# A hybrid decoder layer on one core: buffers and banks laid out anew across three stages, and the first of seven products in three float32r parts

## The chip, the cores and the metric

The kernel runs on one core of a Trainium2 chip. The metric is the device time of one execution in microseconds. Three runs of the kernel before took 2590.86, 2594.02 and 2598.33 us; the median is 2594.02 us.

## The reference

One decoder layer is computed for a prompt of 512 tokens and for 8 samples of 4 tokens, 544 columns in all (NT). The parts that matter here are the dense products:

```
h    = rmsnorm(x) @ w_in           # 2048 -> 6160, split into the heads
y    = concat(o_a, o_b) @ w_out    # gated linear attention | dilated attention
x    = x + y
up   = rmsnorm(x) @ w_ffn_up       # 2048 -> 2 * 5504
conv = causal depthwise conv of width 3 over up; u, g = its two halves
x    = x + (silu(g) * u) @ w_ffn_down
out  = rmsnorm(x)
```

Everything is float32, with states, caches and the last rows of `up` as further outputs.

## The kernel before, in words

**Layout and split products.** Activations lie transposed: 128 features in the partitions, 544 tokens along the row; HT = 272 is half of that. A float32 product is made of float32r matmuls: each operand is split into a high part (ScalarE copies to float32r, L190) and a low part (VectorE subtracts, L191), and three products are added in PSUM: high by high, high by low, low by high (`gemm`, L219 to L226). A weight unit is 8 tiles of 128 x 128 (512 KB): the SP queue loads it into `raw`, `split` makes `whi` and `wlo` from it. A plain product over 16 k has two units and, for two halves of columns, 96 matmuls.

**Who sets the order.** The program is written in Python and a planner orders each engine's instructions by priority and by the times it expects; each engine then runs its list in order. Weight loads and splits stand in `tc.high_priority` (offset PO = 4000), so they are issued ahead of the products that use them, as far as buffers allow. Memory is handed out from two stacks of pools (left and right); a pool opened where another lay waits for the work of the old one.

**The stages.** The in-projection with both attentions fills the time up to about 886 us; its weights go through the pool `wts` (three `raw`, three `whi`, three `wlo`; `wunit`, L196 to L217), its products through the PSUM pool `psg` (two buffers `g` of two banks each), and small products through `pss`. After the last gates (L802 to L805) the attention outputs `o[k]` are split into `og[k]` (L847 to L849, in the order 10 to 15, then 0 to 9). At L810 `wts` is closed and `wu` is opened in its place, with three `raw` and four `whi` and `wlo`.

*Output projection* (L891 to L910): 16 output tiles of 96 matmuls, each added to x (L899), written to `hscr`, squared for the norm, scaled by the norm's weights (L908). For the next stage `factors` (L872 to L888) forms from each pair of tiles (a row pair i, eight in all) seven right-hand blocks: B11, B21, B22 and the sums T1 to T4, each with a high part `vh` and a low part `vl`; four row pairs during the stage, four after it (in `VB`, where the activations lay). B11 is kept as a plain float32 block `v11`.

*Up-projection* (L954 to L1089): 43 pairs f, a tile of the u half and one of the g half. A pair is a 2 x 2 block product done with seven products instead of eight (Strassen's scheme, in Winograd's form) over 8 row pairs, 272 columns each. `p1` is A11 x B11 as 8 full float32 matmuls (`product1`, L941); the other six, `p5`, `p6`, `p2`, `p7`, `p3`, `p4`, are 24 float32r matmuls each (`product`, L934) with a weight split each. The left operands are sums: s = A21 + A22 by a second, adding DMA of the POOL queue (L968); s += A11 on VectorE for p6 (L988); s += A12 for p3 (L998). PSUM holds `b0` (p1, p6, p7, p4 in turn), `z` (p5, p3) and `y` (p2), two buffers each, in `psu`. `p1` of pair f + 1 stands between `p7` and `p3` of pair f; p1 of pair 0 stands in the loop, after the norm's statistics (`rms_stat`, L915) and after `rstdF` and `vcv`. A pair ends with the convolution (L1032 to L1046) and the gated product, which goes to the DRAM scratch `adr`, or stays in SBUF as a kept tile for three pairs.

*Down-projection* (L1093 to L1222): PSUM is opened anew with three buffers `g` and two `v`. First 16 short products of the three kept tiles (18 matmuls), evacuated by ScalarE (L1129), while `fetch` (L1111) brings the other tiles back; then groups of 16, 16 and 8 tiles, the final norm and the output.

Of the kernel before, what the change touches and what calls it, by code (L numbers as in the profile page):

```python
# [9 lines left out]
F32 = mybir.dt.float32  # L10
F32R = mybir.dt.float32r
# [6 lines left out]
P = 128  # L18
# [4 lines left out]
TS = 4  # L23
# [100 lines left out]
def _build(tc, nc, es, xT, st_gla, ck, cv, conv_in, vecs, w_in, w_gu, w_out, w_up, w_dn,  # L124
# [36 lines left out]
    eps = cons.tile([P, 1], F32, name="eps")  # L161
    zs = cons.tile([2 * RANK, NT], F32, name="zs")
    rstd = cons.tile([P, NT], F32, name="rstd")
# [645 lines left out]

    closed(wts_p)  # L810
    wu_p, wu = opened(name="wu", bufs=1, side="right")


    def wsplit(raw, n=8):

        hi = wu.tile([P, 8, P], F32R, tag="whi", name="whi", bufs=4)
        lo = wu.tile([P, 8, P], F32R, tag="wlo", name="wlo", bufs=4)
        split(hi[:, :n], lo[:, :n], raw[:, :n])
        return hi, lo
# [22 lines left out]
    def wraw():  # L842
        return wu.tile([P, 8, P], F32, tag="raw", name="raw", bufs=3)

# [6 lines left out]

    va_p, VA = opened(name="va", bufs=1, side="right")
    hx_p, HX = opened(name="hx", bufs=1, side="right")
    hscr = [dram.tile([P, NT], F32, name=f"hscr{k}") for k in range(KD)]
# [3 lines left out]

    B21, B22, T1, T2, T3, T4 = range(6)
    NV = 6  # L860
    vh, vl, v11 = [None] * (KD // 2), [None] * (KD // 2), [None] * (KD // 2)

# [9 lines left out]
    def factors(some, X, pool):  # L872
        for i in some:
            vh[i] = pool.tile([P, NV, HT], F32R, name=f"vh{i}")
            vl[i] = pool.tile([P, NV, HT], F32R, name=f"vl{i}")
            v11[i] = pool.tile([P, HT], F32, name=f"v{i}")
            nc.scalar.activation(v11[i], X[i][:, 0, :HT], AF.Copy)
        for i in some:
            b11, b12, b21, b22 = X[i][:, 0, :HT], X[i][:, 0, HT:], X[i][:, 1, :HT], X[i][:, 1, HT:]
            t = HX.tile([P, 2, HT], F32, tag="ts", name="ts", bufs=1)  # L880
            u = HX.tile([P, 2, HT], F32, tag="tu", name="tu", bufs=1)
            nc.vector.tensor_sub(t[:, 0], b11, b12)
            nc.vector.scalar_tensor_tensor(t[:, 1], t[:, 0], -1.0, b22, op0=OP.mult, op1=OP.subtract)
            parts(i, T1, 2, t)
            nc.vector.tensor_sub(u[:, 0], b22, b12)
            nc.vector.scalar_tensor_tensor(u[:, 1], t[:, 1], -1.0, b21, op0=OP.mult, op1=OP.subtract)
            parts(i, T3, 2, u)
            parts(i, B21, 2, X[i][:, 1].rearrange("p (a c) -> p a c", a=2))  # L888

    X = {}  # L890
    for ot in range(KD):  # L891
# [17 lines left out]
        if j == 1 and i < AHEAD:  # L909
            factors([i], X, VA)  # L910
    closed(acts_p)
    ra_p, RA = opened(name="ra", bufs=2)
    vb_p, VB = opened(name="vb", bufs=1)
    factors(list(range(AHEAD, KD // 2)), X, VB)
    rms_stat(acc2, rstd, htmp)  # L915
    closed(hx_p, pss, psg)

    g0_p, G0 = opened(name="g0", bufs=NKEPT, side="right")
    fp_p, FP = opened(name="ffn", bufs=1, side="right")
    psu_p, pu = opened(name="psu", bufs=1, space=PSUM)  # L920
    rstdF = FP.tile([P, FW], F32, name="rstdF")
    nc.vector.memset(rstdF, 1.0)
    nc.scalar.activation(rstdF[:, 2:2 + TP], rstd[:, :TP], AF.Copy)
    nc.scalar.activation(rstdF[:, 2 + TP:].rearrange("p (b s) -> p b s", s=2 + TS)[:, :, 2:],
                         rstd[:, TP:].rearrange("p (b t) -> p b t", t=TS), AF.Copy)
    vcv = FP.tile([P, NVEC - V_CW], F32, name="vcv")
    nc.gpsimd.dma_start(vcv, vecs[:, V_CW:])
    wv = w_up.rearrange("(k t p) c -> t p k c", t=2, p=P)
# [11 lines left out]

    def product1(b, a):  # L941
        for i in range(8):
            nc.tensor.matmul(b[:, :HT], a[:, i, :], v11[i], start=(i == 0), stop=(i == 7), skip_group_check=True)  # L943

    def tmp(name):
        return FP.tile([P, HT], F32, tag=name, name=name, bufs=1)

# [6 lines left out]
    class Pair:  # L954
# [5 lines left out]
        def load(self, *parts, tag=None):  # L960

            x = RA.tile([P, 8, P], F32, tag=tag, name=tag) if tag else wraw()
            for n, (side, t) in enumerate(parts):
                c0 = side * FF + self.f * P
                if n == 0:
                    nc.sync.dma_start(x, wv[t][:, :, c0:c0 + P])
                else:
                    nc.gpsimd.dma_start(x, wv[t][:, :, c0:c0 + P], accum_op=OP.add)  # L968
            return x

        def p1(self):
            with ahead():
                self.a11 = self.load((0, 0), tag="ra")
            self.b0 = pu.tile([P, 512], F32, tag="b0", name="b0", bufs=2)
            product1(self.b0, self.a11)
            self.V = tmp("V")
            nc.scalar.activation(self.V, self.b0[:, :HT], AF.Copy)

        def p5(self):
            with ahead():  # L980
                self.s = self.load((1, 0), (1, 1), tag="rs")
                A = wsplit(self.s)
            self.z = pu.tile([P, 512], F32, tag="z", name="z", bufs=2)
            product(self.z, A, T1)
# [9 lines left out]
        def p2(self):  # L994
            with ahead():
                self.a12 = self.load((0, 1))
                A = wsplit(self.a12)
                nc.vector.tensor_add(self.s, self.s, self.a12)  # L998
            y = pu.tile([P, 512], F32, tag="y", name="y", bufs=2)
            product(y, A, B21)  # L1000
# [31 lines left out]
        def conv(self):  # L1032
# [13 lines left out]
            return out  # L1046

    ci_v = conv_in.rearrange("p (s f) r -> p s f r", s=2)
    co_v = conv_out.rearrange("p (s f) r -> p s f r", s=2)
# [5 lines left out]
    ci = co = None  # L1055
    pairs = [Pair(f) for f in range(KF)]
    for f, pr in enumerate(pairs):
# [5 lines left out]
        pr.ci, pr.co = ci[:, :, f % 4, :], co[:, :, f % 4, :]  # L1063
        if f == 0:
            pr.p1()
        pr.p5()
# [20 lines left out]
        if f % 4 == 3 or f == KF - 1:  # L1087
            f4 = f - f % 4
            nc.gpsimd.dma_start(co_v[:, :, f4:f + 1, :], co[:, :, :f + 1 - f4, :])  # L1089
    closed(fp_p, vb_p, ra_p, psu_p)  # L1090


    rows_p, rows = opened(name="rows", bufs=KD)  # L1093
    ds_p, DS = opened(name="ds", bufs=NSLOT)
    psd_p, pg = opened(name="psd", bufs=3, space=PSUM)
    psv_p, pS = opened(name="psv", bufs=2, space=PSUM)

    def vps():
        return pS.tile([P, 512], F32, tag="v", name="v")

    def gps():
        return pg.tile([P, 2, 512], F32, tag="g", name="g")

# [21 lines left out]
    for ot in range(KD):  # L1125
# [3 lines left out]
        nc.scalar.activation(hv(h[ot]), ps[:, :, :HT], AF.Copy)  # L1129
    closed(g0_p, va_p)  # L1130
    ds2_p, DS2 = opened(name="ds2", bufs=24 - NSLOT, side="right")
# [3 lines left out]
    def wraw():  # L1135
        even[0] ^= 1
        if even[0]:
            return wu.tile([P, 8, P], F32, tag="raw", name="raw", bufs=3)
        return W3.tile([P, 8, P], F32, tag="raw3", name="raw3", bufs=2)
# [73 lines left out]
    for s in range(2):  # L1213
# [5 lines left out]
        for ot in range(KD):  # L1219
            eng = nc.gpsimd if ot % 3 == 2 else nc.vector  # L1220
            eng.tensor_mul(h[ot][:, c], h[ot][:, c], rstd[:, c])
            (nc.sync if ot % 2 else nc.scalar).dma_start(yT[ot * P:(ot + 1) * P, c], h[ot][:, c])  # L1222
    closed(w3_p, ds2_p, ds_p, rows_p, wu_p, psv_p, psd_p)

# [65 lines left out]
```

## Time and profile before

| | |
|---|---|
| median of three runs | 2594.02 us |
| the profiled execution | 2600.62 us, span of the profile 2598.8 us |
| mean granted TensorE clock | 0.985 |
| TensorE, VectorE, ScalarE, GpSimd busy | 97%, 60%, 40%, 17% of the span |
| bytes moved by DMA | 427.67 MB, mean 165 GB/s |

PE is TensorE, PEld its weight loads, DVE VectorE, ACT ScalarE, POOL GpSimd, SP the engine that issues most loads; a name with a q (SPq) is an engine's queue of issues. L with a number is a line of the kernel before. The granted clock is a share of 2.4 GHz; 0.50 is the level of 1.2 GHz. A full float32 matmul stands as two records in the trace, a float32r one as one. In rows of the form "out<-in" buffer numbers are left out, so `g` is any of the PSUM buffers of that name.

### The profile page before, as it was taken

The numbers are of one execution on the slowest core, as the hardware profiler recorded it, in microseconds if no ns is written. First come the engines' busy times: TensorE is split into PE (matmuls) and PEld (weight loads), VectorE is DVE, ScalarE is ACT, GpSimd is POOL, SyncE is SP. The second block draws the span as 40 slices with busy tenths as digits, with TensorE's granted clock in tenths as the row PEclk, the third lists the DMA queues.
The fourth block names the chain that finished last, engine by engine and source line by source line (L and its number), as shares of the span: only waits on it lengthen the run. The fifth ranks groups of instructions, "written<-read, shape, count | busy, mean of one in ns | idle before, by whom it ended". The sixth has DMA issues, their size and how long they took to land.

```text
span 2598.8 us, 46302 instructions
## 1 busy us (share of the span) xinstructions
PE 2515.1 (97%) x19135; PEld 2390.4 (92%) x19135; DVE 1570.1 (60%) x2381; ACT 1030.5 (40%) x1777; POOL 452.3 (17%) x592
## 2 busy tenths in 40 slices
PE   7999999999999699979999999999999999999997
PEld 7988877899998599979999999999999999999997
DVE  7877753267767644277777777777777653342244
ACT  5344454133334433244444444444444441131142
POOL 4433333300002300012122212121211000000001
PEclk9999999999999899989999999999999999999999
DMA  7777634622222253379999999999988384353332
GB/s 206 203 204 202 184 108 116 167 75 80 60 77 63 81 148 114 99 164 238 269 242 271 244 268 244 272 243 271 243 185 183 93 242 116 110 157 90 90 90 70
DMA packets 581588, 427.67 MB, mean 165 GB/s; under 512 B 18976, under 2 KB 553728, under 8 KB 580608
## 3 DMA queue, kind: packets, MB, share of 16 engines
q1 hardware_dynamic: 462144, 248.31, 34.7%
q0 software_dynamic: 115200, 171.02, 28.8%
q10 hardware_dynamic: 4032, 5.38, 0.6%
q8 instruction: 150, 2.46, 0.4%
q14 instruction: 62, 0.51, 0.1%
HBM read 397.40 MB, written 77.37 MB: 183 GB/s over the span
## 4 chain that ended last, share of the span: by engine, by line
PE 86%; DMA 6%; DVE 4%; issue 1%; ACT 1%; POOL 0%; SPq 0%; DVEq 0%; POOLq 0%; ACTq 0%
PE g L225 42%; PE b L938 15%; PE z L938 10%; PE b L943 6%; PE y L938 5%; DMA q<-qscr 4%; PE s L660 1%; PE v L507 1%; DMA ar<-adr 1%; PE s L555 1%; PE s L542 1%; DVE pr L411 1%; PE s L778 0%; PE s L781 0%; DMA rs<-in_w_up_dram 0%
## 5 line engine op out<-in xcount | busy, mean ns | idle before, releaser
L190 ACT ACTIVATE whi<-raw 128x1024 fp32r<-128x1024 f32 (+1 forms) x345 | 356.0, 1033 | 702.0 <-PE g L225 470.4
L191 DVE TENSOR_TENSOR wlo<-raw,whi 128x1024 fp32r<-128x1024 f32 (+1 forms) x341 | 408.2, 1198 | 216.7 <-ACT whi L190 208.4
L225 PE MATMUL g<-ah,whi 128*128 128x272 f32 x2048 | 442.4, 295 | 22.2 <-DMA raw<-in_w_out_dram 19.5
L225 PE MATMUL g<-ah,wlo 128*128 128x272 f32 x2048 | 442.9, 294 | 0.3 <-DVE wlo L191 0.3
L225 PE MATMUL g<-al,whi 128*128 128x272 f32 x2048 | 442.9, 295 | 0.0
L225 PEld LDWEIGHTS g<-ah,whi 128*128 128x128 f32 x2048 | 326.6, 190 | 36.9 <-ACT whi L190 22.0
L225 PEld LDWEIGHTS g<-ah,wlo 128*128 128x128 f32 x2048 | 328.1, 191 | 12.2 <-issue 10.1
L225 PEld LDWEIGHTS g<-al,whi 128*128 128x128 f32 x2048 | 327.8, 191 | 12.1 <-issue 10.4
L938 PE MATMUL b<-vh,whi 128*128 128x272 f32 x1032 | 306.3, 297 | 1.3 <-ACT V L1013 1.3
L938 PE MATMUL b<-vh,wlo 128*128 128x272 f32 x1032 | 296.9, 288 | 0.0
L938 PE MATMUL b<-vl,whi 128*128 128x272 f32 x1032 | 296.6, 287 | 0.0
L225 PE MATMUL g<-dh,whi 128*128 128x272 f32 x1248 | 258.5, 289 | 3.3 <-ACT whi L190 2.1
L225 PE MATMUL g<-dl,whi 128*128 128x272 f32 x1248 | 257.9, 288 | 0.0
L225 PE MATMUL g<-dh,wlo 128*128 128x272 f32 x1248 | 257.8, 288 | 0.0
L190 ACT ACTIVATE whi<-rs 128x1024 fp32r<-128x1024 f32 x129 | 135.9, 1054 | 193.8 <-PE b L938 123.6
L191 DVE TENSOR_TENSOR wlo<-rs,whi 128x1024 fp32r<-128x1024 f32 x129 | 157.7, 1222 | 84.5 <-ACT whi L190 84.5
L938 PE MATMUL z<-vh,whi 128*128 128x272 f32 x688 | 207.0, 301 | 0.0
L225 PEld LDWEIGHTS g<-dh,whi 128*128 128x128 f32 x1248 | 195.3, 188 | 4.2 <-ACT whi L190 2.5
L938 PE MATMUL z<-vh,wlo 128*128 128x272 f32 x688 | 198.5, 289 | 0.0
L938 PE MATMUL z<-vl,whi 128*128 128x272 f32 x688 | 198.1, 288 | 0.0
L938 PEld LDWEIGHTS b<-vh,whi 128*128 128x128 f32 x1032 | 194.9, 189 | 3.2 <-ACT V L1013 1.5
L938 PEld LDWEIGHTS b<-vl,whi 128*128 128x128 f32 x1032 | 194.4, 188 | 1.6
(347 smaller groups left out, 4699.0 us busy)
## 6 DMA issues: line engine op xcount, KB each, us to landing
raw<-in_w_up_dram SPq DMA_DIRECT2D x129, 512.0 KB, 5.4
raw<-in_w_in_dram SPq DMA_DIRECT2D x96, 512.0 KB, 4.3
raw<-in_w_dn_dram SPq DMA_DIRECT2D x64, 512.0 KB, 4.2
out_k_s_dram<-in_ck_dram POOLq DMA_DIRECT2D x8, 3060.0 KB, 17.0
out_v_s_dram<-in_cv_dram POOLq DMA_DIRECT2D x8, 3060.0 KB, 17.5
raw<-in_w_up_dram POOLq DMA_DIRECT2D x43, 512.0 KB, 7.7
ra<-in_w_up_dram SPq DMA_DIRECT2D x43, 512.0 KB, 7.6
rs<-in_w_up_dram SPq DMA_DIRECT2D x43, 512.0 KB, 6.4
```

The costliest lines, as they stand in the source:

```text
L190: nc.scalar.activation(hi, src, AF.Copy)
L191: eng.tensor_sub(lo, src, hi.bitcast(F32))
L225: nc.tensor.matmul(ps[:, s, :HT], a, b[:, s * HT:(s + 1) * HT], start=(i == 0 and n == 0), stop=(i == len(todo) - 1 and n == 2))
L411: nc.vector.tensor_mul(pr, kt[:, 4:5, :].broadcast_to([P, TS, QC]), q5[:, 1:5, :])
L507: nc.tensor.matmul(psv[32 * m:32 * m + 32, :QC], lhs, rhs, start=(kt == 0), stop=(kt == 5), tile_position=(0, 32 * m))
L542: nc.tensor.matmul(psc[:, :n], q[r, qi * P:(qi + 1) * P], k[r, :n], start=True, stop=True)
L555: nc.tensor.matmul(psc[r, :P], vt[:, j * P + 64 * e:j * P + 64 * e + 64], t[:, j * P:(j + 1) * P], start=(j == 0), stop=(j == qi))
L660: nc.tensor.matmul(ps[:, c * P:(c + 1) * P], KS[:, c * P:(c + 1) * P], Q[:, :, c * 64:(c + 1) * 64], start=True, stop=True)
L938: nc.tensor.matmul(b[:, :HT], a_[:, i, :], x_[i][:, v, :], start=(first and i == 0 and n == 0), stop=(i == 7 and n == 2), skip_group_check ...
L943: nc.tensor.matmul(b[:, :HT], a[:, i, :], v11[i], start=(i == 0), stop=(i == 7), skip_group_check=True)
```

## The change

1. Weight tiles stay in one pool: `wts` is not closed at L810, and out-, up- and down-projection take `raw`, `whi` and `wlo` from it. The ring of `whi` and `wlo` is three deep there, where `wu` had four. `wu` keeps only p1's and the other products' temporaries `V` and `U`.
2. PSUM: `psg` with its two buffers `g` stays open to the end. `pss` is closed before the output projection and `psu` opened there, with one `v` and two `b0`. In the up-projection z and y are the two halves of one `g`. The down-projection has two `g` where it had three, and one `v` where it had two.
3. B11 is split like the other blocks (seven blocks in `vh` and `vl`), and `p1` becomes a `product` of 24 float32r matmuls with a weight split of A11. `product1` and `v11` go.
4. The tiles `ra` and `rs` of a pair come from `RE` (even pairs) or `RA` (odd pairs), one buffer each, where `RA` had two of each. `RE` is opened on the right before the output projection.
5. `p1` of pair 0 moves ahead of `rms_stat`, and with it ahead of `rstdF` and the load of `vcv`; these now stand after the class `Pair`.
6. `zs` moves from `cons` to `rowsB`.

```diff
-    zs = cons.tile([2 * RANK, NT], F32, name="zs")
+    zs = rowsB.tile([2 * RANK, NT], F32, name="zs", bufs=1)
...
-    closed(wts_p)
     wu_p, wu = opened(name="wu", bufs=1, side="right")
...
-        hi = wu.tile([P, 8, P], F32R, tag="whi", name="whi", bufs=4)
-        lo = wu.tile([P, 8, P], F32R, tag="wlo", name="wlo", bufs=4)
+        hi = wts.tile([P, 8, P], F32R, tag="whi", name="whi")
+        lo = wts.tile([P, 8, P], F32R, tag="wlo", name="wlo")
...
     def wraw():
-        return wu.tile([P, 8, P], F32, tag="raw", name="raw", bufs=3)
+        return wts.tile([P, 8, P], F32, tag="raw", name="raw", bufs=3)
+
+    closed(pss)
+    psu_p, pu = opened(name="psu", bufs=1, space=PSUM)
+
+    def vps():
+        return pu.tile([P, 512], F32, tag="v", name="v")
...
     va_p, VA = opened(name="va", bufs=1, side="right")
+    re_p, RE = opened(name="re", bufs=1, side="right")
     hx_p, HX = opened(name="hx", bufs=1, side="right")
...
-    B21, B22, T1, T2, T3, T4 = range(6)
-    NV = 6
+    B11, B21, B22, T1, T2, T3, T4 = range(7)
+    NV = 7
...
-            v11[i] = pool.tile([P, HT], F32, name=f"v{i}")
-            nc.scalar.activation(v11[i], X[i][:, 0, :HT], AF.Copy)
+            parts(i, B11, 1, X[i][:, 0, :HT].unsqueeze(1))
...
-    ra_p, RA = opened(name="ra", bufs=2)
+    ra_p, RA = opened(name="ra", bufs=1)
     vb_p, VB = opened(name="vb", bufs=1)
     factors(list(range(AHEAD, KD // 2)), X, VB)
-    rms_stat(acc2, rstd, htmp)
-    closed(hx_p, pss, psg)
...
     def tmp(name):
-        return FP.tile([P, HT], F32, tag=name, name=name, bufs=1)
+        return wu.tile([P, HT], F32, tag=name, name=name, bufs=1)
...
-            x = RA.tile([P, 8, P], F32, tag=tag, name=tag) if tag else wraw()
+            x = (RA if self.f % 2 else RE).tile([P, 8, P], F32, tag=tag, name=tag) if tag else wraw()
...
                 self.a11 = self.load((0, 0), tag="ra")
+                A = wsplit(self.a11)
             self.b0 = pu.tile([P, 512], F32, tag="b0", name="b0", bufs=2)
-            product1(self.b0, self.a11)
+            product(self.b0, A, B11)
...
-            self.z = pu.tile([P, 512], F32, tag="z", name="z", bufs=2)
+            self.g = gps()
+            self.z = self.g[:, 0]
             product(self.z, A, T1)
...
-            y = pu.tile([P, 512], F32, tag="y", name="y", bufs=2)
+            y = self.g[:, 1]
             product(y, A, B21)
...
+    pairs = [Pair(f) for f in range(KF)]
+    pairs[0].p1()
+    rms_stat(acc2, rstd, htmp)
+    closed(hx_p)
...
-        if f == 0:
-            pr.p1()
         pr.p5()
...
-    psd_p, pg = opened(name="psd", bufs=3, space=PSUM)
-    psv_p, pS = opened(name="psv", bufs=2, space=PSUM)
```

## Rows read from the trace of the kernel before

**Rows 1.** The page, part 1: busy time of each engine.

```profile
PE 2515.1 (97%) x19135; PEld 2390.4 (92%) x19135; DVE 1570.1 (60%) x2381; ACT 1030.5 (40%) x1777; POOL 452.3 (17%) x592
```

**Rows 2.** Waits of PE: who waited for whom, us in total, times, longest.

```profile
PE g L225 <- DMA raw<-in_w_out_dram: 19.5, 1, 19.5
PE b L943 <- DVE rs L169: 7.7, 1, 7.7
PE v L325 <- DVE acc L906: 7.0, 1, 7.0
```

**Rows 3.** The chain that ended last, both seams: start us, us, what.

```profile
906.03 195.99 PE g L225 x1536
1102.45 5.46 DMA rs<-in_w_up_dram
1109.03 6.44 DMA rs<-in_w_up_dram
1121.67 6.57 PE b L943 x16
1128.24 3.02 PE z L938 x24
```

**Rows 4.** Windows: both holes, the output projection, one pair; busy per engine, clock, DMA.

```profile
core 0: us, PE busy (x) PEld busy (x) DVE busy (x) ACT busy (x) POOL busy (x), PEclk, DMA share, GB/s
...
886.60:906.00 19.40, 0.00 (x0) 0.00 (x0) 7.68 (x14) 3.61 (x7) 9.93 (x13) 0.54 0.65 207
1102.00:1121.70 19.70, 2.58 (x6) 1.03 (x5) 15.26 (x29) 12.26 (x23) 3.72 (x3) 0.62 0.87 174
...
1000.00:1080.00 80.00, 80.00 (x640) 80.00 (x639) 30.68 (x38) 24.68 (x30) 4.46 (x8) 1.00 0.36 107
...
1195.17:1216.90 21.73, 21.73 (x163) 21.10 (x162) 15.55 (x24) 10.03 (x18) 4.57 (x6) 1.00 0.97 233
```

**Rows 5.** The chain inside one pair of the up-projection: start us, us, what.

```profile
1571.94 1.83 PE b L943 x8
1573.77 3.00 PE b L938 x24
...
1590.68 2.99 PE y L938 x24
```

**Rows 6.** Waits of the SP queue's issues: us in total, times, longest.

```profile
SPq L830 <- DVE oa L805: 59.1, 1, 59.1
```

**Rows 7.** Timeline of PE and DVE at the first seam.

```profile
886.16 0.41 PE L764 MATMUL s<-sq,onesV 128*128 128x64 f32 x2 [1.62 <-DVE oa L769]
...
893.00 1.36 DVE L191 TENSOR_TENSOR al<-oa,ah 128x544 fp32r<-128x544 f32 x2
```

**Rows 8.** DVE from 1102 to 1131 us, groups by form: busy, mean ns | idle.

```profile
L870 DVE TENSOR_TENSOR vl<-ts,vh 128x544 fp32r<-128x544 f32 x4 | 2.9, 720 | 1.2 <-ACT vh L869 1.2
...
L882 DVE TENSOR_TENSOR ts<-h 128x272 f32<-128x272 f32 x3 | 1.3, 434 | 0.0
```

**Rows 9.** Groups by form, whole run: the two halves of a weight split.

```profile
L191 DVE TENSOR_TENSOR wlo<-raw,whi 128x1024 fp32r<-128x1024 f32 x325 | 399.3, 1230 | 211.1 <-ACT whi L190 203.0 <-DMA rs<-in_w_up_dram 3.7
L190 ACT ACTIVATE whi<-raw 128x1024 fp32r<-128x1024 f32 x329 | 347.7, 1058 | 691.0 <-PE g L225 467.9 <-PE z L938 153.6 <-PE b L938 16.7
```

**Rows 10.** Waits from 1300 to 1951.6 us (30 pairs of the up-projection).

```profile
ACT whi L190 <- DMA raw<-in_w_up_dram: 0.6, 1, 0.6
```

**Rows 11.** Timeline of ACT and DVE around the end of p3 in one pair.

```profile
1584.92 1.06 ACT L190 ACTIVATE whi<-raw 128x1024 fp32r<-128x1024 f32 x1 [3.66 <-PE z L938]
...
1585.05 0.41 DVE L950 TENSOR_TENSOR F<-z,U 128x240 f32<-128x240 f32 x1 [4.14 <-PE z L938]
...
1586.33 1.22 DVE L191 TENSOR_TENSOR wlo<-raw,whi 128x1024 fp32r<-128x1024 f32 x1
```

**Rows 12.** Timeline of ACT in the products of the kept tiles: fifth and tenth evacuation.

```profile
2073.20 0.61 ACT L1129 ACTIVATE h<-g 128x544 f32<-128x544 f32 x1
...
2087.52 0.61 ACT L1129 ACTIVATE h<-g 128x544 f32<-128x544 f32 x1
```

**Rows 13.** The chain that ended last, where the fetched tiles have come.

```profile
2118.19 442.10 PE g L225 x3532
```

More of the change, by code (lines that the diff above doesn't have):

```diff
@@ L856, in _build @@
     acc2 = HX.tile([P, NT], F32, name="acc2")
-    B21, B22, T1, T2, T3, T4 = range(6)
-    NV = 6
-    vh, vl, v11 = [None] * (KD // 2), [None] * (KD // 2), [None] * (KD // 2)
+    B11, B21, B22, T1, T2, T3, T4 = range(7)
+    NV = 7
+    vh, vl = [None] * (KD // 2), [None] * (KD // 2)
     def htmp(name):
@@ L911, in _build @@
     closed(acts_p)
-    ra_p, RA = opened(name="ra", bufs=2)
+    ra_p, RA = opened(name="ra", bufs=1)
     vb_p, VB = opened(name="vb", bufs=1)
     factors(list(range(AHEAD, KD // 2)), X, VB)
-    rms_stat(acc2, rstd, htmp)
-    closed(hx_p, pss, psg)
[L918 to L927, printed above, removed]
     wv = w_up.rearrange("(k t p) c -> t p k c", t=2, p=P)
@@ L939, in product @@
                                  stop=(i == 7 and n == 2), skip_group_check=True)
-    def product1(b, a):
-        for i in range(8):
-            nc.tensor.matmul(b[:, :HT], a[:, i, :], v11[i], start=(i == 0), stop=(i == 7), skip_group_check=True)
     def tmp(name):
-        return FP.tile([P, HT], F32, tag=name, name=name, bufs=1)
+        return wu.tile([P, HT], F32, tag=name, name=name, bufs=1)
     def second(F, a, b):
@@ L1046, in conv @@
             return out
+    pairs = [Pair(f) for f in range(KF)]
+    pairs[0].p1()
+    rms_stat(acc2, rstd, htmp)
+    closed(hx_p)
+    g0_p, G0 = opened(name="g0", bufs=NKEPT, side="right")
+    fp_p, FP = opened(name="ffn", bufs=1, side="right")
+    rstdF = FP.tile([P, FW], F32, name="rstdF")
+    nc.vector.memset(rstdF, 1.0)
+    nc.scalar.activation(rstdF[:, 2:2 + TP], rstd[:, :TP], AF.Copy)
+    nc.scalar.activation(rstdF[:, 2 + TP:].rearrange("p (b s) -> p b s", s=2 + TS)[:, :, 2:],
+                         rstd[:, TP:].rearrange("p (b t) -> p b t", t=TS), AF.Copy)
+    vcv = FP.tile([P, NVEC - V_CW], F32, name="vcv")
+    nc.gpsimd.dma_start(vcv, vecs[:, V_CW:])
     ci_v = conv_in.rearrange("p (s f) r -> p s f r", s=2)
@@ L1055, in _build @@
     ci = co = None
-    pairs = [Pair(f) for f in range(KF)]
     for f, pr in enumerate(pairs):
@@ L1089, in _build @@
             nc.gpsimd.dma_start(co_v[:, :, f4:f + 1, :], co[:, :, :f + 1 - f4, :])
-    closed(fp_p, vb_p, ra_p, psu_p)
+    closed(fp_p, vb_p, ra_p)
     rows_p, rows = opened(name="rows", bufs=KD)
     ds_p, DS = opened(name="ds", bufs=NSLOT)
-    psd_p, pg = opened(name="psd", bufs=3, space=PSUM)
-    psv_p, pS = opened(name="psv", bufs=2, space=PSUM)
[L1098 to L1102, printed above, removed]
     taken = [0]
@@ L1129, in _build @@
         nc.scalar.activation(hv(h[ot]), ps[:, :, :HT], AF.Copy)
-    closed(g0_p, va_p)
+    closed(g0_p, re_p, va_p)
     ds2_p, DS2 = opened(name="ds2", bufs=24 - NSLOT, side="right")
@@ L1137, in wraw @@
         if even[0]:
-            return wu.tile([P, 8, P], F32, tag="raw", name="raw", bufs=3)
+            return wts.tile([P, 8, P], F32, tag="raw", name="raw", bufs=3)
         return W3.tile([P, 8, P], F32, tag="raw3", name="raw3", bufs=2)
@@ L1222, in _build @@
             (nc.sync if ot % 2 else nc.scalar).dma_start(yT[ot * P:(ot + 1) * P, c], h[ot][:, c])
-    closed(w3_p, ds2_p, ds_p, rows_p, wu_p, psv_p, psd_p)
+    closed(w3_p, ds2_p, ds_p, rows_p, wu_p, wts_p, psu_p, psg)
 def kernel(**inputs):
```

## The prediction

> **What bounds the kernel now.** First the page: TensorE is busy 97% of the span [rows 1], so time can only come from its idle 3% or from matmuls that get cheaper. Second, what TensorE waited for [rows 2]: one wait of 19.5 us for a weight load of the output projection, and two of 7 us and more at the start of the up-projection. Third, the chain that ended last at those two places [rows 3], and the windows around them [rows 4], which show no or hardly any matmul for 19.4 and 19.7 us. Between these two seams TensorE is full. Fourth, the chain inside one pair of the up-projection [rows 5]: six products of 24 float32r matmuls (2.99 to 3.02 us each, 0.1256 us a matmul) and one of full float32 (p1, in two pieces like the row of 1.83 us, 3.66 us together). 6 x 3.01 + 3.66 = 21.7, and in 21.73 us TensorE is busy 21.73, VectorE 15.55, ScalarE 10.03 [rows 4]: the pair has no other limit.
>
> **The change, part by part.**
>
> *Seam 1, in-projection to output projection.* Before, the `wts` pool is closed and `wu` opened where it and its neighbours lay, so the SP queue's first weight load of the new stage waits 59.1 us for the last L805 of the gates [rows 6], and TensorE starts at 906.03 [rows 3]; its last work of the old stage was at 886.16 [rows 7]. After, `wts` stays open, and the first units of w_out are loaded and split while the last in-projection products run. What is late next is the split of the last activation tiles: `og[8]` and `og[9]`, whose VectorE part ends at 893.00 + 1.36 = 894.36 [rows 7]. The order of k puts 8 and 9 last, so 14 of 16 k can run earlier. Two to four weight splits now stand on VectorE in front of that chain, 1.23 us each [rows 9], so I put its end at 898. Twelve matmuls are then left of the first output tile, 1.5 us: it ends at 899.5. Before, it ended at 921.2: 906.03, 96 matmuls at 0.1256 us, and 3.1 us lost by the start at the 1.2 GHz level (the granted clock of the hole is 0.54 [rows 4]); the 3.1 is the 195.99 us of this stage's 1536 matmuls [rows 3] less 1536 x 0.1256. Gain 21 us; bounds 10 (the first loads still wait for something of the gates) and 25 (no split in front).
>
> *Seam 2, output projection to up-projection.* Before, the loads of pair 0 start when the last output tile is done (1102.45), the added second load follows at 1109.03 because it must wait for the first, and TensorE resumes at 1121.67 with p1, at the 1.2 GHz level: 6.57 us [rows 3] instead of 3.66. After, pair 0 loads into `RE` and `wts` during the output projection, and p1, on its own PSUM bank and ahead of the norm's statistics, needs only its B11 parts: 4 x 2 short operations after 1102. So p1 costs nothing here. Late next are the factors T1 of the last four row pairs. On VectorE each takes three `vl` at 0.72 and four sums at 0.434 us [rows 8], 3.9 us. Three whole ones (11.7), the last one's T1 (2 x 0.434 + 0.72 = 1.6), four B11 subtractions (1.7) and the last addition to h (0.72) make 15.7 us: T1 is complete at 1117.8 and p5 ends near 1118.5, against 1131.26 before (1128.24 + 3.02 [rows 3]). From these 12.8 us I take 3 for a start at the lower clock level, as at seam 1. The statistics, `rstdF` (one VectorE and two ScalarE operations) and the POOL queue's load of `vcv` move behind p1; `rstd` is first read after p7 and `vcv` by the convolution, 12 us later and more. Gain 10 us; bounds 0 (statistics and weight splits keep their place in front of the factors, as they do now) and 20 (the whole hole).
>
> *The pairs.* p1 becomes 24 float32r matmuls: 3.02 instead of 3.66 us, 0.64 to 0.65 a pair; 42 pairs (pair 0's p1 is in seam 2) give 27 us. Added per pair: one split, 1.06 us on ScalarE and 1.23 us on VectorE [rows 9]. Loads with new sums are ScalarE 11.1 and VectorE 16.8 of 21.1 us, both below TensorE. No DMA is added: the load of a11 was there and only moves to `RE`/`RA` by turns, two buffers of each kind as before; SP and POOL issue the same list. ScalarE waits only 0.6 us in 650 for a raw tile [rows 10], so the loads have room for a pair that is 3% shorter. ScalarE's split now waits at its queue's head for a buffer three products back, and behind it stand the evacuations of p1, p6 and p7; TensorE needs those one product later at the earliest.
>
> The rows show fp32 at 3.66 and the three parts at 3.02, a ratio of 0.83. The Trainium skill, FP8 and Floating Point Precision, section TensorE Precision Notes, counts four passes through the array for true fp32, so three parts would be three quarters, an estimate of 2.75 us; 42 x 0.91 would give 38 us instead of 27. The rows decide for 27, since 24-matmul products of the same shapes already run in this stage.
>
> *The smaller ring.* `whi`/`wlo` go from four buffers to three while splits per pair go from six to seven. What covers this is the lead of the splits. The shortest lead I find in a pair is p2's: its ScalarE half starts at 1584.92, having waited for the product p3 to release a buffer, VectorE ends at 1586.33 + 1.22 = 1587.55 [rows 11], the product starts at 1590.68 [rows 5]: 3.1 us. One buffer fewer costs one product, 3.0 us, of lead. So the cover just holds. Lower bound 0; upper bound one split exposed per pair, 2.29 us. I take 0, being nearer to the row with its 3.1 us, and keep the other for a rival.
>
> *Down-projection.* `g` goes from three buffers to two. The output projection runs with two already, and 80 us of it hold 80 us of matmuls [rows 4]; so the long groups cost nothing. The 16 short products of the kept tiles (18 matmuls, 2.27 us) are different: their evacuations stand on ScalarE behind splits of fetched tiles that wait for DMA. The fifth evacuation starts at 2073.20, the tenth at 2087.52 [rows 12], 14.3 us for five instead of 11.3, so they fall behind by 3 us, more than a second buffer covers (2.27). Bounds 0 (the 16th fetch, which ends this stretch at 2118.19 [rows 13], hides it) and 6; I take 3 us lost.
>
> *Edits at nothing:* `zs` in another pool, p1's `V` and `U` in `wu`, z and y as halves of one `g`: both were double before, and y is read long before its tile is wanted again.
>
> **Sum** against the profiled execution (2600.6 us, span 2598.8): -21 - 10 - 27 + 3 = -55, 2545.6. The median of the runs shown, 2594.0, lies 6.6 below that execution; so 2539 us.
>
> **The rivals.**
>
> *The ring eats the cheaper p1.* The pairs stay at 21.73 us because the split, not the matmul, now sets the pace. For it: the lead of 3.1 us against a loss of 3.0, and VectorE in order, which already stands 4.14 us a pair waiting for p3 [rows 11]. Against: 4.3 us a pair of VectorE still free. Time: 2539 + 27 = 2566. The same number comes out if the DMA engines, busy for 0.97 of such a pair [rows 4], cannot deliver in 21.1 us.
>
> *One split exposed per pair: slower.* Place: the up-projection, where s += a11 stands between the splits of p5 and p6 on the same buffer, and three products in flight hold all three buffers. Price: 1.06 + 1.23 = 2.29 us x 42 = 96; 2539 + 96 = 2635, 41 above now. It turns the sign from 55 / 42 = 1.3 us a pair on. Against it: TensorE has no gap at all in this stage now, and the in-projection ran with three buffers, though with products of 6 us.
>
> *The seams do not close.* If the moved pools only exchange one wait for another (h tiles, PSUM, pool space), 31 us are missing: 2570. For it: SP's wait was for L805, which is late anyway. Against: three weight buffers that never close have nothing to wait for but their own products.
>
> *Three passes instead of four.* If p1's 24 matmuls ran closer together than those of the other six products do, down to three quarters of 3.66 us, the sum would be 2528; the 2.99 to 3.02 us rows of the same shape [rows 5] speak against it. The page that counts four passes is named above.
>
> **How the numbers follow.** Forecast 0.60 (2539, its own range 2527 to 2553 from the bounds of seams and kept tiles taken together); ring or DMA eats p1: 0.15 (2566); seams stay: 0.05 (2570); three passes: 0.04 (2528); partial exposure beyond 2573: 0.09, a little of it within the 0.3% (8 us) that a measurement of this kernel can tell from no change; one split a pair: 0.07 (2635). The range 2526 to 2573 holds 0.84. Faster 0.91, same 0.02, slower 0.07.
>
> **What would show it.** Right: no wait of TensorE for w_out; the first output tile done near 900; p1 before the statistics; pairs of 21.1 us with seven products of 3.02; evacuations L1129 at most 3 us late. Wrong: rows of TensorE waiting for `whi` or `wlo` in the up-projection, a pair above 21.4 us, or a hole at 1102 that is still longer than 15 us.

## The result and the profile after

The changed kernel takes 2561.57 us (median of 4 runs, 2555.30 to 2567.31), the kernel before, run beside it, 2595.40 (2590.86 to 2598.33): a ratio of 0.9871 with a 95% interval from 0.9842 to 0.9899, so 1.3% or 34 us faster. The forecast was 2539, its range 2526 to 2573. The profiled executions, which the stages below compare, lie further apart: the spans are 2598.8 and 2553.5, 45.3 us. One run of this study, 3425.09 us at a granted clock of 0.652 (the first kernel with the last products in `b0`), is left out of its ratio.

The ends of the stages, read from the two timelines (us from the start of the span), with two of the experiments beside them:

| | before | after | ring of three alone | half copies |
|---|---|---|---|---|
| last matmul of the in-projection's products | 879.4 | 874.0 | 872.8 | 873.7 |
| first output tile done | 921.2 | 890.7 | 895.0 | 890.4 |
| output projection done | 1102.0 | 1071.5 | 1075.8 | 1071.2 |
| first pair done | 1147.7 | 1105.5 | 1120.6 | 1106.5 |
| up-projection done | 2060.7 | 2011.8 | 2030.9 | 1992.7 |
| span | 2598.8 | 2553.5 | 2571.4 | 2531.4 |

"First pair done" is the moment at which as many matmul records have run behind the output projection as a pair has (160 before, 168 after), since TensorE takes pieces of neighbouring pairs between each other.

Of the 45.3 us, 5.4 lie in the in-projection, where the two kernels hardly differ (it ends anywhere from 872 to 879 us in the profiles whose in-projection has no copies, so this is scatter), 25.1 at seam 1, 11.7 at seam 2 (45.7 to 34.0 from the end of the output projection to the end of the first pair), 6.7 in the 42 further pairs, and 3.6 were lost from there to the end. Before's first 160 records hold two `p1`, about 1.7 us more work than a pair's own (3.66 us against 16 x 0.1256); counted by equal work, an estimate, seam 2 gives some 10 us and the pairs some 8.

In the rows of a run, L counts the lines of that run's own kernel. The page of after, part 1, against [rows 1]: the same share for TensorE from less work, and one split more per pair for VectorE and ScalarE.

```profile
PE 2483.1 (97%) x19479; PEld 2384.3 (93%) x19479; DVE 1625.9 (64%) x2432; ACT 1063.8 (42%) x1820; POOL 459.4 (18%) x592
```

The waits of TensorE in after, against [rows 2]: the 19.5 us for `w_out` are gone. A wait that before did not have heads the list, for the ScalarE half of p7's split; the last one comes from the two `g`.

```profile
PE b L931 <- ACT whi L190: 15.6, 12, 2.9
...
PE g L225 <- DVE h L1188: 1.8, 1, 1.8
```

Windows of after (columns as in [rows 4]): the 19.4 us of the old first hole are full, and so are four early pairs; in 500 us of the middle, 13.8 are idle. The last line is before's for the same 500 us, without idle time.

```profile
886.60:906.00 19.40, 19.40 (x157) 19.40 (x157) 12.11 (x19) 6.31 (x9) 8.54 (x14) 1.00 0.71 232
1171.80:1255.80 84.00, 84.00 (x673) 84.00 (x673) 67.32 (x93) 42.83 (x77) 17.49 (x24) 1.00 1.08 259
1300.00:1800.00 500.00, 486.24 (x3841) 484.05 (x3840) 385.39 (x527) 247.35 (x437) 109.78 (x141) 0.99 1.07 254
```

```profile
1300.00:1800.00 500.00, 500.00 (x3683) 485.46 (x3682) 357.70 (x506) 230.81 (x414) 103.51 (x138) 1.00 1.08 256
```

The chain that ended last in after, from the first seam into the pairs (start us, us, what). The four `b` rows lie 22.04, 42.93 and 44.03 us apart: an undisturbed pair takes 21.0. Twelve of the sixteen pairs beside a copy (below) are 0.4 to 3.0 us longer; in such a pair the chain leaves TensorE for two loads in a row.

```profile
888.63 182.62 PE g L225 x1454
...
1243.84 8.64 PE b L931 x69
...
1265.88 8.95 PE b L931 x69
...
1285.37 13.91 DMA raw<-in_w_up_dram
1299.86 6.79 DMA raw<-in_w_up_dram
1308.81 8.96 PE b L931 x69
...
1328.30 13.90 DMA raw<-in_w_up_dram
1342.76 7.93 DMA raw<-in_w_up_dram
1352.84 8.96 PE b L931 x69
```

These are p7's loads: A11 by the SP queue, then A21 added to it by POOL's, which waits for the first. POOL's and ScalarE's timelines show the rest (idle time and its releaser in brackets): POOL issues a copy of an attention cache (3060 KB, DRAM to DRAM, one in every second pair) at 1272.79; the first load runs beside it, and POOL stands 8.83 us for it; ScalarE then stands 3.68 us for the sum.

```profile
1272.79 1.23 POOL L1088 DMA_DIRECT2D out_v_s_dram<-in_cv_dram  x1
1274.52 1.62 POOL L957 DMA_DIRECT2D rs<-in_w_up_dram  x1 [0.50 <-issue]
...
1299.86 1.60 POOL L957 DMA_DIRECT2D raw<-in_w_up_dram  x1 [8.83 <-DMA raw<-in_w_up_dram]
```

```profile
1306.75 1.06 ACT L190 ACTIVATE whi<-raw 128x1024 fp32r<-128x1024 f32 x1 [3.68 <-DMA raw<-in_w_up_dram]
```

In pairs without a copy the first load takes 4 to 5.5 us and both together 11 to 15.6; with one, 11.5 to 14.6 and 19.6 to 23.5. The four pairs beside a copy whose chain takes 19.6 to 20.1 us show no gap, the twelve with 20.9 to 23.5 do. Before had the same pattern, 8.8 to 10.6 us for the first load and 16 to 20 for both, in pairs of 21.7.

The order of POOL's issues differs too. After issues the copy ahead of the second load of `rs` (p5's sum for the next pair), as above, and so it does at all sixteen copies; before issued it behind:

```profile
1576.55 1.58 POOL L968 DMA_DIRECT2D rs<-in_w_up_dram  x1 [1.57 <-DVE rs L988]
...
1578.10 1.23 POOL L1086 DMA_DIRECT2D out_v_s_dram<-in_cv_dram  x1
```

So in after two transfers of POOL's are still moving when p7's first load is issued at 1285.37: the copy, which lands at 1290.08, and the load of `rs`, which lands at 1295.59. In before that load has landed by then. The issues from 1268 to 1330 us in before and in after (KB each, median us from issue to landing):

```profile
rs<-in_w_up_dram POOLq DMA_DIRECT2D x3, 512.0 KB, 10.9
```

```profile
rs<-in_w_up_dram POOLq DMA_DIRECT2D x3, 512.0 KB, 20.4
```

The theory after the result: the chain of two loads through one slot of the `raw` ring has become longer than a pair (A). The rivals: the ring of three split buffers is short by a product (B), or the DMA engines are full (C).

### The profile page after: what moved, and what is told of

The parts are those of the page before. It is cut to its first block, busy times and chain, and to the rows that moved or that the text cites. A ratio compares the mean times of both kernels' runs of the same rounds, so it can differ in the third digit from the quotient of the medians.

```text
span 2553.5 us, 47085 instructions
## 1 busy us (share of the span) xinstructions
PE 2483.1 (97%) x19479; PEld 2384.3 (93%) x19479; DVE 1625.9 (64%) x2432; ACT 1063.8 (42%) x1820; POOL 459.4 (18%) x592
## 4 chain that ended last, share of the span: by engine, by line
PE 76%; DMA 13%; DVE 5%; issue 2%; ACT 1%; POOL 0%; DVEq 0%; ACTq 0%; SPq 0%; POOLq 0%
PE g L225 43%; PE b L931 15%; PE g L931 10%; DMA raw<-in_w_up_dram 9%; DMA q<-qscr 4%; PE s L660 1%; PE v L507 1%; PE s L555 1%; PE s L542 1%; DVE wlo L191 1%; ACT whi L190 1%; DVE pr L411 1%; PE s L778 1%; PE s L781 0%; DVE h L1215 0%
## 5 line engine op out<-in xcount | busy, mean ns | idle before, releaser
L931 PE MATMUL b<-vh,whi 128*128 128x272 f32 x1376 | 397.6, 290 | 16.4 <-ACT whi L190 15.6
L931 PE MATMUL b<-vl,whi 128*128 128x272 f32 x1376 | 397.0, 289 | 0.0
L931 PE MATMUL b<-vh,wlo 128*128 128x272 f32 x1376 | 390.6, 289 | 0.0
L225 PEld LDWEIGHTS g<-ah,wlo 128*128 128x128 f32 x2048 | 326.2, 189 | 11.5 <-issue 10.1
L931 PE MATMUL g<-vh,whi 128*128 128x272 f32 x1032 | 298.1, 289 | 2.9 <-ACT vh L875 2.9
L931 PE MATMUL g<-vl,whi 128*128 128x272 f32 x1032 | 299.1, 290 | 1.3 <-DVE vl L876 1.3
L931 PE MATMUL g<-vh,wlo 128*128 128x272 f32 x1032 | 296.7, 287 | 0.0
L931 PEld LDWEIGHTS b<-vh,whi 128*128 128x128 f32 x1376 | 260.9, 190 | 19.3 <-ACT whi L190 18.2
L931 PEld LDWEIGHTS b<-vl,whi 128*128 128x128 f32 x1376 | 260.5, 189 | 0.0
L931 PEld LDWEIGHTS b<-vh,wlo 128*128 128x128 f32 x1376 | 258.2, 189 | 0.0
```

Of the source, the lines that this page charges most:

```text
L225: nc.tensor.matmul(ps[:, s, :HT], a, b[:, s * HT:(s + 1) * HT], start=(i == 0 and n == 0), stop=(i == len(todo) - 1 and n == 2))
L931: nc.tensor.matmul(b[:, :HT], a_[:, i, :], x_[i][:, v, :], start=(first and i == 0 and n == 0), stop=(i == 7 and n == 2), skip_group_check ...
```

## The experiments

Ratios are to the kernel before, run beside each (medians 2591.7 to 2594.1).

**The cache copies moved out of the pairs.** Three tries at putting the same sixteen copies elsewhere; `copy` issues the next one, and in the first two tries its calls stand in the turns of the gated linear attention, in the third in the groups of the down-projection.

```diff
-        if f % 2 == 1 and f < 4 * NB:
-            b, (src, dst) = f // 4, ((ck, k_s), (cv, v_s))[f // 2 % 2]
-            tc.keep_in_program_order(nc.gpsimd.dma_start(dst[b, 0:PAST - TS, :], src[b, TS:PAST, :]))
...
+            copy(1)
```

> The changed kernel with its 16 cache copies issued during the linear attention, not in the pairs. Theory A (load chain: p7's two loads one after the other, lengthened by a copy in flight, come too late for a split that now leads its product by one product less): no pair above 21.1 us, TensorE's waits for whi in the up-projection from 15.6 us to under 2, the whole 15 to 22 us less than the changed kernel, ratio to before 0.979 to 0.982. Theory B (a seventh split on ScalarE and VectorE with three buffers stalls TensorE, copies or not): the long pairs stay, ratio 0.986 to 0.988. A third way: the copies slow the linear attention's weight loads and the gain is given back there, ratio 0.985 or more with pairs of 21.0 us.

2704.37 us, ratio 1.043 (1.0416 to 1.0444): the whole is slower. Without a fixed place, the planner put all sixteen at the very start, as nothing holds them there, and TensorE stood behind the first weights, as its waits show:

```profile
PE s L341 <- DVE wz L191: 160.5, 1, 160.5
```

But all pairs took 21.0 us, and the up-projection lost its 22 us of gaps. The second try pins the copies to the attention's turns:

> As the first run with moved copies, but with the copies held in program order, three or four beside each of the five turns of the linear attention. Theory A: pairs of 21.0 us as in that run, the in-projection ends within 5 us of the changed kernel, ratio 0.978 to 0.982. Rival: bursts of four copies slow the weight loads of the in-projection, whose end moves by 20 us or more; ratio 0.986 or above.

2560.17 us, ratio 0.9881 (0.9865 to 0.9896). Pairs 21.0 throughout, the up-projection some 22 us shorter, and 28 us lost in the in-projection, 17.3 of them in the longest of its waits at the start of the attention's scan (us in total, times, longest):

```profile
PE s L660 <- DVE QB L656: 19.5, 2, 17.3
```

The third moves them to the down-projection:

> The changed kernel with the 16 copies beside every second output tile of the first two groups of the down-projection, 24 us apart. Theory A: pairs of 21.0 us; the groups of 16 tiles keep 12.0 us an output tile since two weight loads of 4 us are needed in 12; ratio 0.978 to 0.982. Rival: the copies stretch the loads there as they do in the pairs, and 10 us or more are lost in the groups; ratio 0.984 or above.

2689.74 us, ratio 1.0379 (1.0363 to 1.0396): the copies were issued from the end of the up-projection on, eight of them within 5 us and the rest every 10, and held up the weights of the kept tiles:

```profile
PE g L225 <- ACT whi L190: 145.0, 8, 57.8
```

All three agree on the pairs: no copies, no gaps. B falls, as the ring is the same in them; A and C stay.

**p1 in full float32 again, the layout kept.**

```diff
-                A = wsplit(self.a11)
...
-            product(self.b0, A, B11)
+            product1(self.b0, self.a11)
```

> The changed kernel with p1 as eight full float32 matmuls again, everything else of the change kept. By the forecast's sum p1 was worth 27 us: 28 us slower than the changed kernel, ratio to before 0.997 to 0.999. By theory A the stalls go too, since a pair is 0.7 us longer and has a split less in the ring: pairs of 21.7 us throughout, 10 to 14 us slower than the changed kernel, ratio 0.991 to 0.993.

2581.92 us, ratio 0.9959 (0.9945 to 0.9973), between the two ranges expected. So the layout alone gives 0.4%, and p1's three parts the rest, 0.9871 - 0.9959 = 0.9%, some 23 us. The pairs are 22.1 here, longer than before's 21.73: in each one the chain goes through ScalarE's split of a weight (1.06 us, most of it beside p1's last matmuls), and some 0.4 us are uncovered. It isn't the ring of three alone, as the next run shows; what else in the layout does it was not separated. The chain in one pair:

```profile
1253.49 2.65 PE b L932 x21
1256.13 0.02 issue
1256.15 1.06 ACT whi L190
1257.22 0.04 issue
1257.26 0.52 PE g L932 x2
```

**The kernel before with a ring of three, nothing else.**

```diff
-        hi = wu.tile([P, 8, P], F32R, tag="whi", name="whi", bufs=4)
-        lo = wu.tile([P, 8, P], F32R, tag="wlo", name="wlo", bufs=4)
+        hi = wu.tile([P, 8, P], F32R, tag="whi", name="whi", bufs=3)
+        lo = wu.tile([P, 8, P], F32R, tag="wlo", name="wlo", bufs=3)
```

> The kernel before with three whi and wlo buffers instead of four, nothing else. Theory A (the lead lost by the smaller ring lets late loads show): some pairs with a copy above 21.8 us, 3 to 15 us slower, ratio 1.001 to 1.006. Theory B (it takes the seventh split): no pair longer than 21.8, ratio 1.000 within 0.001.

2575.07 us, ratio 0.9932 (0.9918 to 0.9946): one buffer fewer makes the kernel before 17 us faster, which neither theory foresaw. From the last in-projection matmul to the first output tile it takes 22.2 us, where before took 41.9 and after takes 16.7. The SP queue's 59.1 us for L805 [rows 6] are gone; of that kind, 7.5 for an earlier tile of the same name are left, and the chain shows the first load of `w_out` at 873.97, where before had it at 897.98:

```profile
SPq L830 <- DVE oa L769: 7.5, 1, 7.5
```

```profile
873.97 5.30 DMA raw<-in_w_out_dram
879.35 1.06 ACT whi L190
880.44 1.24 DVE wlo L191
```

The reason fits the sizes: with rings of three, three and three, `wu` has 9 tiles of 4 KB per partition, as `wts` had; with four it has 11 and reaches 8 KB into the memory of the pool beside it, which the gates still used. That the reach was into just those tiles is argued, not shown. Seam 2 stays at 44.8 us here, the pairs at 21.7.

**`wts` closed and opened again in the changed kernel.**

```diff
+    closed(wts_p)
+    wts_p, wts = opened(name="wts2", bufs=3, side="right")
```

> The changed kernel, but with the weight pool closed and opened anew at the start of the output projection, as before. If that pool alone opened seam 1: TensorE has a hole of 15 us or more before the output projection again, and its first output tile ends 22 to 27 us later than in the changed kernel. If the PSUM pools or the place of the other tiles did it: at most 5 us later.

2553.14 us in one run. The stretch to the first output tile is 22.1 us, as with the ring alone, 5.4 more than in after: the pool alone did not open the seam. So the ring's size alone gives 19.7 of the 25.1 us of seam 1, and the pool that stays open adds 5.4 to that. What it would give with a ring of four was not run.

**A split buffer of p1's own.** Kept tiles share one buffer to make room.

```diff
-                A = wsplit(self.a11)
+                if self.f:
+                    A = FP.tile([P, 8, P], F32R, name="hi1", bufs=1), FP.tile([P, 8, P], F32R, name="lo1", bufs=1)
+                    split(A[0], A[1], self.a11)
+                else:
+                    A = wsplit(self.a11)
```

> The changed kernel with a split buffer of p1's own (one whi and one wlo beside the ring of three, so that six splits share the ring as in the kernel before's and the seventh has its own). To make room the three kept tiles of the down-projection share one buffer: two of the three kept products are left out of the output's sense, not of the time. If the lead lost by the ring lets the late loads show: waits for whi in the up-projection from 15 to 23 us down to under 5, ratio 0.980 to 0.983. If p7's load chain alone is too long for its buffer: waits of 10 us and more remain, ratio 0.985 to 0.988.

2557.02 us, ratio 0.9864 (0.9847 to 0.9881). The gaps stay: TensorE waits 12.8 us for `whi` in the pairs.

```profile
PE g L931 <- ACT whi L190: 12.8, 15, 2.4
```

The ring's lead is not what is missing. The waits have moved, though: the product is now p5 (it writes `g`), and the chain there runs through p7's two loads and then the second load of `rs`, 21.8 us behind a copy.

**Two buffers of p7's own for its sum.**

```diff
-                A = wsplit(self.load((0, 0), (1, 0)))
+                A = wsplit(self.load((0, 0), (1, 0), tag="r7"))
...
+            x = FP.tile([P, 8, P], F32, tag=tag, name=tag, bufs=2) if tag == "r7" else (RA if self.f % 2 else RE).tile([P, 8, P], F32, tag=tag, name=tag) if tag else wraw()
```

> The changed kernel with two buffers of their own for p7's sum of two loads, so that the chain of 20 to 23 us has two pairs of time instead of one; the copies stay in the pairs. The three kept tiles share one buffer here too, for room. Theory A with the chain of p7 as the late part: no pair above 21.2 us, ratio 0.979 to 0.982, though not a byte less is moved. If the copies delay other loads as much (rs, p2's): long pairs remain, ratio 0.984 to 0.987.

2545.89 us, ratio 0.9825 (0.9809 to 0.9841). With every copy in its place and the same bytes, the middle window is full but for 1.6 us, at a higher rate than after's 254 GB/s:

```profile
1300.00:1800.00 500.00, 498.44 (x3976) 497.26 (x3975) 396.09 (x544) 256.08 (x450) 110.68 (x142) 1.00 1.11 265
```

So the engines can deliver in pairs of 21.0, and C falls; what was late is the chain of two loads, which may start only when its slot is free. The two buffers also take p7's loads out of the `raw` ring, so the run doesn't tell p7's slots from a longer `raw` ring. The ratio lies above the range expected because seam 2 takes 45 us here: pair 0's p7 loads into the pool `ffn`, which opens behind the statistics, and its first load starts at 1093.15.

**Half copies.** The other way to mend the chain needs no memory.

```diff
-        if f % 2 == 1 and f < 4 * NB:
+        if f < 4 * NB:
             b, (src, dst) = f // 4, ((ck, k_s), (cv, v_s))[f // 2 % 2]
-            tc.keep_in_program_order(nc.gpsimd.dma_start(dst[b, 0:PAST - TS, :], src[b, TS:PAST, :]))
+            HR = (PAST - TS) // 2
+            r0 = f % 2 * HR
+            tc.keep_in_program_order(nc.gpsimd.dma_start(dst[b, r0:r0 + HR, :], src[b, TS + r0:TS + r0 + HR, :]))
```

> The changed kernel, with each 3 MB copy of the caches cut in two halves, one half issued in each pair below 32 instead of a whole one in every second pair. The bytes, the queue and the last issue stay as they were. Theory A (a copy that is still moving when p7's first load is issued stretches that load from 4 or 5 us to 11 to 15 us, so that p7's chain of two loads takes 20 to 23 us, longer than a pair of 21.0): a whole copy moves for 14 us and more, half of one for some 7 to 9, so it has ended before the next pair's first load; p7's chain falls below 18 us, all pairs take 21.0 to 21.3, the up stage is 15 to 22 us shorter, and the ratio to the kernel before is 0.979 to 0.983 (2540 to 2549 us). Rival B (what counts is the bytes that move in two pairs, and the pairs run out of transfer time): the same 20 to 23 us of waits are spread over all 32 pairs, which take 21.6 to 21.8 each, and the ratio stays at 0.986 to 0.989.

2533.21 us, ratio 0.9783 (0.9759 to 0.9806), a little better than A's range. The waits for `whi` in the pairs fall from 15.6 to 0.7 us and the up-projection from 940.3 to 921.5. The chain of two loads now fits, but not for the reason that A gave: a half is still moving when the next pair's first load starts (in the pair shown above it is issued at 1275.72 and lands at 1288.03; the load is issued at 1285.41). What the halves do is spread the delay: beside them the first load takes 6.4 to 10.8 us in every pair instead of 4 to 5.5 and 11.5 to 14.6 by turns, the chain 15 to 20.5: not always below 18, but no longer than a pair. In that pair POOL can issue the second load at 1294.91, for a first one issued at 1285.41:

```profile
1294.91 1.58 POOL L957 DMA_DIRECT2D raw<-in_w_up_dram  x1 [7.88 <-ACT co L1029]
```

```profile
PE b L931 <- ACT whi L190: 0.7, 3, 0.3
```

```profile
1300.00:1800.00 500.00, 499.27 (x3984) 498.40 (x3983) 399.80 (x547) 256.84 (x451) 112.03 (x152) 1.00 1.11 264
```

**Pair 0's p1 written behind the statistics again.**

```diff
-    pairs[0].p1()
     rms_stat(acc2, rstd, htmp)
+    pairs[0].p1()
```

> The changed kernel, with pair 0's p1 moved back behind the reciprocal root mean square (rms_stat) and nothing else. If the 11.7 us of the second seam came from p1's place ahead of that chain, the first pair ends 5 to 10 us later than in the changed kernel (34.0 us behind the end of the output projection there, 39 to 44 here), with TensorE idle before p1. If they came from the loads that can start earlier or from the other buffers alone, the first pair ends within 2 us of 34.0.

2546.30 us in one run, and seam 2 takes 33.9 us. But TensorE's list is the same: p1 still starts at 1069.39, right behind the last output product, with the statistics after it. The planner puts p1 there whatever its line, as soon as nothing of the statistics stands in its way. So the run doesn't test p1's place on TensorE; it shows that the line which moved is not what placed it. In before, `psu` could only open after `psg` and `pss` had closed behind the statistics; a bank that is open earlier is the likely cause, and whether that or `RE` is needed was not separated.

**The last products in other banks.** The products of the last eight output tiles' halves (the expectations call them the last two) go to the two `b0`, then by turns to two `g` and two `b0`, with the half copies.

```diff
-            ps = gps()
+            ps = pu.tile([P, 512], F32, tag="b0", name="b0", bufs=2).unsqueeze(1)
```

> The changed kernel, with the products of the last two tiles' halves in two banks of their own name (b0, free by then) instead of the two g buffers, and nothing else. If the last stage became 2.0 us longer because g has two buffers instead of more, so that TensorE waits for VectorE's evacuation, which stands behind the output's own multiplies (g L225 <- DVE h L1188): the last stretch of products falls from 27.0 to 25 us, that wait is gone, and the span is 1.5 to 2.5 us shorter (ratio to the kernel before 0.0006 to 0.001 below that of the changed kernel, which the timing can hardly tell; the stretch in the profile decides). If the longer stretch comes from the order of the output's multiplies alone, it stays at 27 us.

2562.14 us, ratio 0.9873 (0.9852 to 0.9894); the stretch stays at 26.96 us and the wait at 1.7. Two other banks are again two, so this could not tell the number from the order. Four can:

```diff
+            ps = pu.tile([P, 512], F32, tag="b0", name="b0", bufs=2).unsqueeze(1) if ot % 2 else gps()
```

> The kernel with the half copies, and the products of the last two tiles' halves by turns in a g buffer and in a b0 bank: four in turn instead of two (the run with two b0 banks had two as well, and its last stretch stayed at 26.96 us with a wait of 1.7 us for L1188). If the number of buffers is the cause: between the end of the first halves and the end of the last product 25 us instead of 27, no wait of TensorE for L1188, and 2531.4 - 2 = about 2529.5 us of span in a profiled execution like the half copies' own; ratio to the kernel before 0.9765 to 0.979. If the order of VectorE alone is the cause, 27 us and the half copies' ratio, 0.978.

The stretch is 24.9 us (2495.97 to 2520.90) and the wait is gone: the number of buffers is the cause. The whole takes 2538.59 us, ratio 0.9782 (0.9768 to 0.9797); against the half copies' 0.9783 two microseconds cannot be told in the time. Both beat the changed kernel by 0.9%.

## Why the prediction was right, and where it was not

The sign and the range were right; the likeliest time was 23 us too low. In the profiles, which lie 45.3 us apart where the medians lie 34, the pairs gave 20 us less than forecast and seam 1 gave 4 more. The range held only because it was drawn to take in a rival at 2566: the forecast's own range, 2527 to 2553, was missed.

*Seam 1* (forecast: 21, bounds 10 and 25): 25.1 in the profiles. The size was nearly right, the cause not the one that was needed, so the near hit is in part luck. "After, `wts` stays open" was given as what ends the wait for L805; a ring of three, which the prediction treated only as a risk in the pairs, gives 19.7 us with `wts` closed as before, and the open pool adds 5.4. The rival of moved pools that exchange one wait for another missed it too.

*Seam 2* (forecast: 10): 11.7, or some 10 by equal work. Before, TensorE stood 7.0, 2.4 and 7.7 us for the statistics and for p1 behind them; after, p1 and parts of p5 and p6 run first, and it waits 7 us in short pieces while VectorE makes the factors: in 1071.4 to 1105.5 VectorE is busy 28.7 of 34.1 us. The reading that the factors come late next held; p5 ends 21.1 us behind the output projection, where before it ended 29.3 behind and the forecast with its 3 us for the clock had 19.5. The seam in after:

```profile
1071.40:1105.50 34.10, 26.96 (x173) 24.35 (x172) 28.70 (x50) 20.91 (x39) 7.38 (x9) 0.85 0.59 131
```

The 173 matmuls would take 21.7 us at 0.1256 each; they take 26.96 at a mean granted clock of 0.85 (0.50 for 10.24 us of it). So the lower clock costs about 5 us there by this estimate, where 3 were forecast.

*The pairs* (forecast: 27): 6.7, or some 8 by equal work. The price of p1 was right, even low: undisturbed pairs are 21.01, 0.72 below 21.73, 30 us in 42. Some 22 of them went again into the gaps of p7: 16 us of idle TensorE (15.6 of it the twelve waits for `whi`), and about 3 because the granted clock was 0.50 for 3.4 us behind two of these waits (2.8 and 2.7 us long; behind one of 3.0 it stayed at 1.00). The remaining 3 us were not traced.

The step that failed is that the loads were taken as they were. The sentence "ScalarE waits only 0.6 us in 650 for a raw tile [rows 10], so the loads have room for a pair that is 3% shorter" reads slack from the consumer; a wait near nought says that a load is in time, not by how much. Read from the loads, p7's two took 16 to 20 us beside a copy in before. That might still have fitted: chains of up to 20.1 us leave no gap in after, and the half copies run pairs of 21.1 on chains of up to 20.5. But the chain itself grew, to 19.6 to 23.5. "SP and POOL issue the same list" holds for the transfers, not for their order: POOL's copy moved ahead of the second load of `rs`. The ring of three alone has that order too, and there the chain takes 18.4 to 20.2 us in pairs of 21.7, without gaps. How much of the growth is due to the order, and how much to the shorter pair, was not tried.

Of the rivals the one with the DMA engines was nearest, at 2566 against 2562, but not by its cause: the engines had the rate, as the runs with two slots and with half copies show, and two loads in a row through one slot beside a large copy did not fit.

*The smaller ring* (forecast: nothing in the pairs): right, as p1's own buffer did not help and pairs of 21.0 and of 21.7 ran on three; only the 0.4 us a pair with p1 in float32 stay unexplained. The rival of one split exposed in every pair fell with it.

*The down-projection*: from the last product of the up-projection to the last of the kept tiles it takes 39.5 us instead of 37.2, so 2.4 lost for 3 forecast. Two `g` alone do not explain them: the half copies, with the same two, take 37.4. That "the long groups cost nothing" overlooked the last stretch: VectorE runs eleven output products (6.6 us) ahead of two evacuations, in before as well, but there a third `g` kept TensorE going, 24.9 us for the stretch instead of 27.0. Price 2.1 us, given back by two more banks. The chain of after at that place:

```profile
2519.13 6.55 DVE h L1215 x11
2526.43 12.30 PE g L225 x96
```

*Four passes*: the Trainium skill, FP8 and Floating Point Precision, section TensorE Precision Notes, counts four passes for true fp32, hence 2.75 us for p1 as an estimate. The trace does not bear the estimate out: three parts take 3.00 us against 3.66, a ratio of 0.82. A quarter of a full float32 matmul is 114 ns here (3.66 us by 8 by 4), and a float32r matmul takes 125; how many passes a full one makes, no run here shows.

## What to carry to other kernels

Before a stage is made shorter, read each of its loads from the release of its slot to its landing and compare the longest with the new period; a consumer's wait of nought hides how close it is. Compare the order of each queue's issues too, not only the list. Large transfers without a deadline are best cut into pieces and spread, so that the longest chain beside them stays below the period (up to 20.5 us beside half copies, 23.5 beside whole ones, for a pair of 21.0). A buffer more in one ring can cost more at a pool's border than it gives, 17 us here. A transfer that depends on nothing may be issued long before its line suggests: three of these runs moved the same copies, and the two in which they were issued in a row lost 4%.

## What was not expected of the hardware

In the up-projection of after a 512 KB load (p7's first) takes 4 to 5.5 us in pairs without a copy and 11.5 to 14.6 while a 3060 KB copy from DRAM to DRAM, issued on another queue, still moves; beside half such a copy, 6.4 to 10.8. The Trainium skill, Trainium Kernel Development and Optimization, section Key Constraints, says that transfers issued from the SP, ScalarE and GpSimd queues run on the same 16 engines and interleave; these rows agree. With the copies cut in halves the same pairs moved 264 GB/s instead of 254. Why the first load beside a whole copy takes 11.5 us and more in after, and 8.8 to 10.6 in before, was not tried; the order on POOL's queue is a difference that the rows show. With the ring of three alone, which has after's order and before's p1, it takes 10.2 to 12.1.
